# A decoder layer on one core: attention's transposes over four banks, block one's softmax after block zero's, and rooms for the raw weights of sevenfold chunks

## The chip, the cores and the metric

The kernel runs on one core of a Trainium2 chip. The metric is the device time of one execution in microseconds (us); less is better. TensorE is PE (its weight loads PEld), VectorE DVE, ScalarE ACT, GpSimd POOL, SyncE SP. DMAs are issued from SP's and ACT's queues.

## The reference

One layer of a hybrid decoder, 256 tokens of width 2048, float32. Cut to what matters:

```python
h = rmsnorm(x, norm_mix_pre)
xr, yr, q, k, v, g_rnn, g_attn = split(h @ w_in)
y_rnn = rg_lru(conv(xr)) * gelu(yr)
y_att = sliding_window_sink_attention(rope(q), rope(k), v, sinks)   # 32 heads of 64, 4 key heads
mix = sigmoid(g_rnn) * (y_rnn @ w_rnn_proj) + sigmoid(g_attn) * (y_att @ w_attn_proj)
x = x + rmsnorm(mix @ w_out, norm_mix_post)
u = square(relu(rmsnorm(x, norm_mlp_pre) @ w_mlp_up))               # 2048 -> 8192
x = x + rmsnorm(u @ w_mlp_down, norm_mlp_post)                      # 8192 -> 2048
```

The attention works in two blocks of 128 queries; block zero sees its own 128 keys, block one 256.

## The kernel before, in words

**Weights.** Every weight matrix comes in chunks of 128 x 2048, each as two halves of 128 x 1024 (512 KB). A float32 product is made of three single-pass products: a weight w is split into whi = w rounded (a cast on ACT, line 94) and wlo = w - whi (DVE, line 95), and so are the activations. The class Stream (lines 54 to 156) does this in the order of use. load_to (66 to 78) issues the raw halves from SP into a ring of WRAW = 4 tiles named wraw; split_to (80) splits them into rings of six whi and six wlo; ahead (138 to 140) keeps the splitting six halves and the loading four more ahead of the half that PE uses.

**Rooms.** A pool named big has 12 rooms of 128 x 2048 float32 with the tag U8. hT, h2T (four rooms each), x, the rooms of the scores, uT, acc and others take them in turn: a tile that asks for a room waits until the one that had it before is no longer used.

**Attention** (532 to 636), for four groups g of eight query heads. It is a generator: a pass of PE over weights calls pump, which moves it on to its next yield, so its small matmuls stand between the weight matmuls. scores (549 to 570) makes the products q.k, and on DVE adds the mask and takes the maximum of each tile. softmax (572 to 590) subtracts the maximum with the exponential on ACT (582, with an accumulating read) and scales on DVE (587). turn_probs (592 to 607) transposes the probabilities on PE (604), four to a PSUM bank, and ACT copies them out; there are two such banks (psm). Then come the products with v (630). In the order before, the scores of both blocks are made and masked first, and then softmax(0) and, after a yield, softmax(1).

**First norm** (433 to 449). r = 1/rms of the tokens is spread over the partitions by a matmul of ones with a diagonal (448, tile pr), and copied to rT. keys_values (515 to 528) calls it, rotates and turns the keys (tile pk).

**MLP.** The hidden width is done in two parts f = 0 and 1. In each, 16 pairs p of up-projection steps (a_pair or up_pair) and evacuate (1063) make uT, of which the pairs in SEVEN = (0, 2, ... 12) are kept in a special form of seven left operands (tiles "seven", pool pc). Then down (1092) makes the product with w_dn in two passes n of 1024 output columns. A chunk of a pair in SEVEN is a "sevenfold" chunk: four 128 x 128 by 512 products are made from seven instead of eight (a Winograd form). For that split_sums (114 to 136) forms sums of the raw weights on DVE: t (123), then two sums of 512 (125, 126), the two halves' whi and wlo, thi on ACT (129) and tlo on DVE (130). t, thi and tlo take big rooms. PE uses 21 matmuls of 512 columns for a sevenfold chunk and 24 for a plain one (1084); they alternate up to p = 12, then three plain ones end the pass. todo (980) is a list of up-projection steps that PE does ahead between the transposes of the second norm.

**End.** In the last pass (f = 1, n = 1) early (1190) adds acc, the sum of the earlier parts, to the four results of the sevenfold products: two on DVE and two on POOL. It also asks for x1, the residual, back from DRAM. between (1199) multiplies the finished columns by the gain g3, finish (1205) adds the last bank, squares (1214), norms, and writes out (1223, 1224).

The order of instructions on each engine comes from the tile framework's scheduler, with priorities, and from "pin", which keeps the program's order.

Of the kernel before, what the change touches and what calls it, by code (L numbers as in the profile page):

```python
# [30 lines left out]
NH, NKV, HD = 32, 4, 64  # L31
# [5 lines left out]
WRAW, WHALF, T2, HELD = 4, 6, 8, 4  # L37

SEVEN = (0, 2, 4, 6, 8, 10, 12)
# [14 lines left out]
class Stream:  # L54
# [11 lines left out]
    def load_to(self, n):  # L66
        while self.loaded < min(n, 2 * len(self.chunks)):
            j = self.loaded
            c = slice(j % 2 * 1024, j % 2 * 1024 + 1024)
            if j < 2 * EXTRA:  # L70
                if j % 2 == 0:
                    self.place = self.room(f"wraw{j}")
                t = self.place[:, c]
            else:
                t = self.pool.tile([P, 1024], F32, tag="wraw", bufs=WRAW, name=f"wraw{j}")
            self.nc.sync.dma_start(t, self.chunks[j // 2][:, c])
            self.raw[j] = t
            self.loaded += 1

# [57 lines left out]

    def ahead(self, j):
        self.split_to(j + AHEAD)
        self.load_to(max(2 * EXTRA, j + WHALF) + WRAW)  # L140

    def half(self, run_ahead=True):
        j = self.at
# [20 lines left out]
EXTRA = 5  # L164


def layer(tc, x, g_pre, pos_t, pos_row, inv_freq, vecs, sinks, gains, w_kv, w_q, w_xy, w_rg, w_g, w_rp, w_ap, w_out,
          w_up, w_dn, out):
    nc = tc.nc
# [8 lines left out]
    mm = nc.tensor.matmul  # L178
# [43 lines left out]
    def bank(pool, name):  # L222
        return pool.tile([P, 512], F32, tag=pool.name, name=name)
# [105 lines left out]
    def quarter(q):  # L329
        return slice(q * 512, q * 512 + 512)  # L330
# [13 lines left out]
    ident = const.tile([P, P], F32, name="ident")  # L344
# [3 lines left out]
    sq = const.tile([P, 4, TB, 4], F32, name="sqs")  # L348
    ones = const.tile([P, P], F32, name="ones")
# [80 lines left out]
    ws.ahead(ws.at - 1)  # L430
    r0, r0h = [], []
    rT = pa.tile([P, S], F32, name="rT")

    def first_norm():

        pr = bank(psm, "pr")
        spread = t2("spread")
        for tb in range(TB):
            r = rms(tb, 0)
            half = st[:, 16 + tb : 17 + tb]  # L440
            nc.vector.tensor_scalar(half, r, 0.5, None, ALU.mult)
            r0.append(r)
            r0h.append(half)
            for t in (cc, ss):
                nc.vector.tensor_scalar(t[:, tb], t[:, tb], r, None, ALU.mult)
            dg = spread[:, tb * P : tb * P + P]
            nc.vector.tensor_scalar(dg, ident, r, None, ALU.mult)
            mm(pr[:, tb * P : tb * P + P], ones, dg, start=True, stop=True)
        nc.scalar.copy(rT, pr[:, 0:S])

    pos_i = pa.tile([P, TB], I32, name="pos_i")
# [63 lines left out]
    def keys_values(banks):  # L515
        yield
        first_norm()
        for tb in range(TB):
            nc.scalar.activation(v_sb[:, tb, :], banks[tb][:, 256:512], AF.Copy, scale=r0[tb])
            k2 = t2("k2")  # L520
            k4 = k2.rearrange("p (g c d) -> p g c d", g=NKV, c=2)
            rope(banks[tb][:, 0:256], tb, NKV, [k4[:, :, 0, :], k4[:, :, 1, :]])
            yield
            ps = bank(psm, "pk")
            for g in range(NKV):
                nc.tensor.transpose(ps[:, g * P : g * P + P], k2[:, g * P : g * P + P], ident)
            nc.scalar.copy(kT[:, :, tb * P : tb * P + P], ps.rearrange("p (g t) -> p g t", g=NKV))
            yield

    yatt = []  # L530

    def attention(g, banks):

        qT = pa.tile([P, 4, S], F32, tag="qT", bufs=2, name=f"qT{g}")
        for tb in range(TB):
# [3 lines left out]
            ps = bank(psm, "pq")  # L539
# [6 lines left out]
        rooms, stats, tiles = {}, {}, {}  # L546
# [42 lines left out]

        pT = {}  # L590

        def turn_probs(tb):
            nk = 1 + tb
            per = 4 // nk
            if tb:
                room_p = flat(unit("pT", F32)).rearrange("p (n c) -> p n c", c=512)
            else:
                room_p = rooms[tb][:, 2:4, :]
            for par in range(2):
                for kb in range(nk):  # L600
                    ps = bank(psm, "pt")
                    for h in range(4):
                        s3, at = tiles[tb][h // per * 2 + par]
                        nc.tensor.transpose(ps[:, h * P : h * P + P], s3[:, h % per, kb * P : kb * P + P], ident)
# [20 lines left out]
        yield  # L625
# [213 lines left out]
    x1 = po.tile([P, TB, D], F32, name="x1")  # L839
# [40 lines left out]
    held = o_pass(mixT, banks, HELD)  # L880
# [208 lines left out]

    PLACE = {(0, 0): "Q4", (0, 1): "Cs", (1, 0): "P2", (1, 1): "Q3"}  # L1090

    def down(f, n, uT, held, order, finish, early, between=lambda p: None):
# [21 lines left out]
        for p in range(PAIRS - held):  # L1114
# [25 lines left out]
                        begun.add(b)  # L1140
            between(p)
        parts = [[ws.half(False) for i in range(2)] for p in range(held)]
        for name in order:
            for i in range(held):
                step(PAIRS - held + i, parts[i], (name,))
            finish(name, banks[PLACE[name]], ready[name])
        ws.ahead(ws.at - 1)

    for f in range(2):
# [38 lines left out]
        x1 = []  # L1188

        def early(ready):  # L1190
            for (tb, i), t in ready.items():
                c = quarter(2 * n + i)
                (nc.gpsimd if n and tb else nc.vector).tensor_tensor(t, t, acc[tb][:, c], ALU.add)
            if n == 1:
                for tb in range(TB):
                    x1.append(flat(unit(f"x1{tb}", F32)))
                    nc.scalar.dma_start(x1[tb], x1_away[tb])

        def between(p):
            if p in (3, 5, 7, 9):  # L1200
                tb, q = divmod((p - 3) // 2, 2)
                c = quarter(q)
                nc.vector.tensor_tensor(acc[tb][:, c], acc[tb][:, c], g3[:, c], ALU.mult)

        def finish(name, b, t):
            tb, i = name
            q = 2 * n + i
            c = quarter(q)
            a = acc[tb][:, c]
            nc.vector.tensor_tensor(a, b, t, ALU.add)  # L1210
# [3 lines left out]
            nc.scalar.activation(spare[:, c], a, AF.Square, accum_out=sq[:, 3, tb, q : q + 1])  # L1214
            nc.vector.tensor_tensor(t, a, g3[:, quarter(q)], ALU.mult)
            last[tb, i] = t
            if i == 0:
                return
            r = rms(tb, 3)
            for q in range(4):  # L1220
                c = quarter(q)
                g = acc[tb][:, c] if q < 2 else last[tb, q - 2]
                nc.vector.scalar_tensor_tensor(x1[tb][:, c], g, r, x1[tb][:, c], ALU.mult, ALU.add)
                (nc.scalar if q % 2 else nc.sync).dma_start(o_v[tb][:, c], x1[tb][:, c])

        n = 0
        down(f, n, uT, 2, order, finish, early)
        n = 1
        last = {}
        spare = flat(unit("spare", F32))  # L1230
        g3 = flat(unit("g3", F32))
        nc.scalar.dma_start(g3, gains[3].partition_broadcast(P))
        down(f, n, uT, 2, [(0, 0), (0, 1), (1, 0), (1, 1)], finish, early, between)
    ctx2.close()
    ctx.close()

# [71 lines left out]
```

## Time and profile before

| | |
|---|---|
| three runs | median 1517.41 us (1516.36 to 1518.62) |
| profiled execution | 1517.5 us |
| its span | 1515.7 us |
| weights from DRAM | 288.60 MB read, 195 GB/s over the span |
| granted TensorE clock | 1.00 in all stretches up to 1500 us |

A row of a group has the line, engine, operation, out<-in, shapes and count, then busy time and mean duration in ns, and last the idle time of that engine just before them with what ended most of it. A row of a timeline has start, duration, engine, line and operation, and in brackets the idle time before it and its releaser.

### The profile page before, as it was taken

How to read it: one execution, taken by the hardware profiler on the slowest of the kernel's cores; microseconds unless marked ns; L12 is line 12 of the kernel's file. 1: busy time of each engine (PE TensorE's matmuls, PEld its weight loads, DVE VectorE, ACT ScalarE, POOL GpSimd, SP SyncE). 2: the span in 40 equal slices, each digit the busy share in tenths (PEclk: the TensorE clock that was granted, in tenths of full speed). 3: DMA queues.
4: the chain of work that ended last, by engine and by line, in shares of the span. 5: the costliest groups of instructions: out<-in, count | busy, mean ns of one | idle time of the engine just before them, and what ended most of it. 6: DMA issues, size and time to landing. Idle time of an engine off the chain costs nothing.

```text
span 1515.7 us, 20016 instructions
## 1 busy us (share of the span) xinstructions
PE 1493.5 (99%) x7600; PEld 1259.8 (83%) x7600; DVE 1102.2 (73%) x1377; ACT 829.2 (55%) x1143; POOL 5.5 (0%) x11
## 2 busy tenths in 40 slices
PE   9999999999999999999999999999999999999996
PEld 7787778788888888888888888888888888888875
DVE  6666677858769966555667866798886666688897
ACT  6554654646566766443355655555454455555543
POOL 0000000000000000000000000000000000000001
PEclk9999999999999999999999999999999999999999
DMA  6645445465646565655764756566657555566564
GB/s 253 218 144 187 142 131 170 153 196 166 217 159 215 174 209 196 191 183 194 268 225 137 271 183 193 185 203 213 219 195 239 194 188 188 193 236 213 195 209 174
DMA packets 82895, 296.19 MB, mean 195 GB/s; under 512 B 9712, under 2 KB 9968, under 8 KB 81648
## 3 DMA queue, kind: packets, MB, share of 16 engines
q1 hardware_dynamic: 79056, 284.43, 57.4%
q10 hardware_dynamic: 3744, 10.50, 1.9%
q8 instruction: 59, 0.97, 0.2%
q14 instruction: 36, 0.29, 0.1%
HBM read 288.60 MB, written 6.29 MB: 195 GB/s over the span
## 4 chain that ended last, share of the span: by engine, by line
PE 82%; DVE 9%; DMA 4%; ACT 2%; issue 2%; DVEq 0%; SPq 0%; ACTq 0%
PE ps L256 21%; PE ps L254 11%; PE dQ L1084 4%; DMA wraw<-in_w_dn 4%; PE pp L294 4%; PE pp L296 4%; PE pp L298 4%; PE g L294 3%; DVE wlo L95 3%; PE g L298 3%; PE g L296 3%; PE s L1084 3%; PE dP L1084 2%; PE q L296 2%; PE q L298 2%; PE q L294 2%
## 5 line engine op out<-in xcount | busy, mean ns | idle before, releaser
L94 ACT CAST whi<-wraw 128x1024 fp32r<-128x1024 f32 x523 | 544.6, 1053 | 567.5 <-PE ps L256 123.7
L95 DVE TENSOR_TENSOR wlo<-wraw,whi 128x1024 fp32r<-128x1024 f32 x523 | 632.8, 1221 | 301.9 <-ACT whi L94 295.2
L256 PE MATMUL ps<-h2T,whi 128*128 128x512 f32 x960 | 223.9, 390 | 0.0
L256 PEld LDWEIGHTS ps<-h2T,whi 128*128 128x128 f32 x960 | 178.2, 188 | 35.6
L256 PE MATMUL ps<-hT,whi 128*128 128x512 f32 x512 | 121.3, 391 | 0.0
L254 PEld LDWEIGHTS ps<-h2T,wlo 128*128 128x128 f32 x960 | 119.1, 192 | 2.3
L254 PE MATMUL ps<-h2T,wlo 128*128 128x256 f32 x960 | 119.9, 283 | 0.0
L256 PEld LDWEIGHTS ps<-hT,whi 128*128 128x128 f32 x512 | 94.7, 188 | 20.1 <-issue 1.5
L1084 PE MATMUL dQ<-whi,uT 128*128 128x512 f32 x288 | 106.9, 389 | 0.0
L294 PE MATMUL g<-whi,hT 128*128 128x512 f32 x256 | 101.2, 395 | 0.0
L296 PE MATMUL g<-wlo,hT 128*128 128x512 f32 x256 | 100.0, 391 | 0.1
L298 PE MATMUL g<-whi,hT 128*128 128x512 f32 x256 | 99.8, 390 | 0.0
L254 PE MATMUL ps<-hT,wlo 128*128 128x256 f32 x512 | 64.9, 283 | 0.0
L254 PEld LDWEIGHTS ps<-hT,wlo 128*128 128x128 f32 x512 | 63.8, 191 | 1.2
L1084 PEld LDWEIGHTS dQ<-whi,uT 128*128 128x128 f32 x288 | 54.1, 188 | 11.2
L1084 PE MATMUL dQ<-wlo,uT 128*128 128x512 f32 x144 | 56.4, 391 | 1.2 <-DVE wlo L95 1.1
L294 PEld LDWEIGHTS g<-whi,hT 128*128 128x128 f32 x256 | 48.1, 188 | 10.6 <-issue 1.0
L298 PEld LDWEIGHTS g<-whi,hT 128*128 128x128 f32 x256 | 48.1, 188 | 10.2
L296 PEld LDWEIGHTS g<-wlo,hT 128*128 128x128 f32 x256 | 48.1, 188 | 9.9 <-DVE wlo L95 0.5
L1084 PE MATMUL dCs<-whi,uT 128*128 128x512 f32 x144 | 54.1, 389 | 0.0
L1084 PE MATMUL dP<-whi,uT 128*128 128x512 f32 x144 | 54.1, 389 | 0.0
L130 DVE TENSOR_TENSOR tlo<-t,thi 128x1536 fp32r<-128x1536 f32 x28 | 49.2, 1756 | 5.5 <-ACT thi L129 5.3
(280 smaller groups left out, 2462.1 us busy)
## 6 DMA issues: line engine op xcount, KB each, us to landing
wraw<-in_w_up SPq DMA_DIRECT2D x128, 512.0 KB, 4.1
wraw<-in_w_dn SPq DMA_DIRECT2D x128, 512.0 KB, 4.8
wraw<-in_w_g SPq DMA_DIRECT2D x64, 512.0 KB, 4.7
wraw<-in_w_xy SPq DMA_DIRECT2D x64, 512.0 KB, 4.5
wraw<-in_w_q SPq DMA_DIRECT2D x32, 512.0 KB, 4.4
wraw<-in_w_ap SPq DMA_DIRECT2D x32, 512.0 KB, 4.6
wraw<-in_w_rp SPq DMA_DIRECT2D x32, 512.0 KB, 4.1
wraw<-in_w_out SPq DMA_DIRECT2D x32, 512.0 KB, 4.9
```

Of the source, the lines that this page charges most:

```text
L94: self.pin(self.nc.scalar.copy(hi, src))
L95: self.pin(self.nc.vector.tensor_tensor(lo, src, hi.bitcast(F32), ALU.subtract))
L130: v.tensor_tensor(lo, t, hi.bitcast(F32), ALU.subtract)
L254: mm(ps[:, f, 1, :], w, a[:, 0, :], start=False, stop=j == 1 and k == 7)
L256: mm(ps[:, f].rearrange("p a b -> p (a b)"), w, a.rearrange("p a b -> p (a b)"), start=kt == 0, stop=j == 3 and k == 7)
L294: mm(banks[tb][n], a[:, 0, t], hi[:, n * 512 : n * 512 + 512], start=first, stop=False)
L296: mm(banks[tb][n], a[:, 0, t], lo[:, n * 512 : n * 512 + 512], start=False, stop=False)
L298: mm(banks[tb][n], a[:, 1, t], hi[:, n * 512 : n * 512 + 512], start=False, stop=last)
L1084: mm(b, a[x], w[y], start=not begun and i == 0, stop=tail and i == 2)
```

## The change

In Stream, the raw halves of sevenfold chunks (in self.sums) no longer come from the ring of four but from one big room for both halves, in all four passes of the down projection. ahead loads in such a way that the two halves of a sevenfold chunk go together. In the attention softmax(0) goes ahead of the scores of block one; in the first three groups the transposes of block zero come one step of the pump earlier, and block one's 16 go together, over four banks (a pair of banks and the two of psm); in the last group block zero's come later and block one's in two bundles. The spreading of r goes behind the transposes of the keys, in a function of its own. 30 instead of 26 up-projection steps stand ahead of the first turn of the second norm. In the last pass all four adds of early are on DVE, x1 comes back on SP's queue behind the last weights, in four pieces, g3 in two halves on ACT's queue, both in rooms of "seven" tiles no longer used; the squares are written to the PSUM bank itself.

```diff
-            if j < 2 * EXTRA:
+            if j < 2 * EXTRA or j // 2 in self.sums:
                 if j % 2 == 0:
                     self.place = self.room(f"wraw{j}")
                 t = self.place[:, c]
...
     def ahead(self, j):
         self.split_to(j + AHEAD)
-        self.load_to(max(2 * EXTRA, j + WHALF) + WRAW)
+        n = max(2 * EXTRA, j + WHALF) + WRAW
+
+        self.load_to((n + 1) // 2 * 2 + 2 if (n - 1) // 2 in self.sums else n)
...
+    def spread_out():
+        pr = bank(psm, "pr")
+        for tb in range(TB):
+            mm(pr[:, tb * P : tb * P + P], ones, spread[:, tb * P : tb * P + P], start=True, stop=True)
         nc.scalar.copy(rT, pr[:, 0:S])
...
         scores(0, 0, [bank(psm, "sc") for par in range(2)])
+        softmax(0)
         scores(1, 0, [bank(psb, "sc") for par in range(2)])
         if not last_group:
             scores(1, 1, two_banks("sc"))
-        softmax(0)
         yield
         if last_group:
             scores(1, 1, [bank(psb, "sc") for par in range(2)])
         softmax(1)
         yield
-        turn_probs(0)
         yield
-        yield
-        turn_probs(1)
-        yield
+        if last_group:
+            yield
+            turn_probs(0)
+            yield
+            yield
+            yield
+            turn_probs(1, (0,))
+            yield
+            turn_probs(1, (1,))
+            yield
+            yield
+        else:
+            turn_probs(0)
+            yield
+            yield
+            turn_probs(1, banks=two_banks("pt"))
+            yield
...
-    for q, n in enumerate((26, 6, 6, 6)):
+    for q, n in enumerate((30, 6, 6, 6)):
...
-                (nc.gpsimd if n and tb else nc.vector).tensor_tensor(t, t, acc[tb][:, c], ALU.add)
-            if n == 1:
-                for tb in range(TB):
-                    x1.append(flat(unit(f"x1{tb}", F32)))
-                    nc.scalar.dma_start(x1[tb], x1_away[tb])
+                nc.vector.tensor_tensor(t, t, acc[tb][:, c], ALU.add)
...
         def between(p):
-            if p in (3, 5, 7, 9):
+            if p in (0, 2):
+                g3.append(free_half(f"g3{p}"))
+                nc.scalar.dma_start(g3[-1], gains[3][p * 512 : p * 512 + 1024].partition_broadcast(P))
+            if p in (4, 6, 8, 10):
...
+        def residual_back():
+
+            for tb in range(TB):
+                for i in range(2):
+                    x1[tb, i] = free_half(f"x1{tb}{i}")
+                    with tc.issue_after(ws.load):
+                        ws.load = nc.sync.dma_start(x1[tb, i], x1_away[tb][:, i * 1024 : i * 1024 + 1024]).ins
```

More of the change, by code (lines that the diff above doesn't have):

```diff
@@ L75, in load_to @@
                 t = self.pool.tile([P, 1024], F32, tag="wraw", bufs=WRAW, name=f"wraw{j}")
-            self.nc.sync.dma_start(t, self.chunks[j // 2][:, c])
+            self.load = self.nc.sync.dma_start(t, self.chunks[j // 2][:, c]).ins
             self.raw[j] = t
@@ L432, in layer @@
     rT = pa.tile([P, S], F32, name="rT")
+    spread = t2("spread")
     def first_norm():
-        pr = bank(psm, "pr")
-        spread = t2("spread")
         for tb in range(TB):
@@ L445, in first_norm @@
                 nc.vector.tensor_scalar(t[:, tb], t[:, tb], r, None, ALU.mult)
-            dg = spread[:, tb * P : tb * P + P]
-            nc.vector.tensor_scalar(dg, ident, r, None, ALU.mult)
-            mm(pr[:, tb * P : tb * P + P], ones, dg, start=True, stop=True)
+            nc.vector.tensor_scalar(spread[:, tb * P : tb * P + P], ident, r, None, ALU.mult)
+    def spread_out():
+        pr = bank(psm, "pr")
+        for tb in range(TB):
+            mm(pr[:, tb * P : tb * P + P], ones, spread[:, tb * P : tb * P + P], start=True, stop=True)
         nc.scalar.copy(rT, pr[:, 0:S])
@@ L517, in keys_values @@
         first_norm()
+        keys = []
         for tb in range(TB):
             nc.scalar.activation(v_sb[:, tb, :], banks[tb][:, 256:512], AF.Copy, scale=r0[tb])
-            k2 = t2("k2")
-            k4 = k2.rearrange("p (g c d) -> p g c d", g=NKV, c=2)
+            keys.append(t2("k2"))
+            k4 = keys[tb].rearrange("p (g c d) -> p g c d", g=NKV, c=2)
             rope(banks[tb][:, 0:256], tb, NKV, [k4[:, :, 0, :], k4[:, :, 1, :]])
             yield
+        yield
+        yield
+        for tb in range(TB):
             ps = bank(psm, "pk")
             for g in range(NKV):
-                nc.tensor.transpose(ps[:, g * P : g * P + P], k2[:, g * P : g * P + P], ident)
+                nc.tensor.transpose(ps[:, g * P : g * P + P], keys[tb][:, g * P : g * P + P], ident)
             nc.scalar.copy(kT[:, :, tb * P : tb * P + P], ps.rearrange("p (g t) -> p g t", g=NKV))
-            yield
+        yield
+        spread_out()
+        yield
     yatt = []
@@ L590, in attention, with turn_probs @@
         pT = {}
-        def turn_probs(tb):
+        def turn_probs(tb, pars=(0, 1), banks=()):
             nk = 1 + tb
             per = 4 // nk
[L595 to L599, printed above, removed]
+            if pars[0] == 0:
+                rooms["p", tb] = (flat(unit("pT", F32)).rearrange("p (n c) -> p n c", c=512) if tb
+                                  else rooms[tb][:, 2:4, :])
+            room_p = rooms["p", tb]
+            banks = list(banks)
+            for par in pars:
                 for kb in range(nk):
-                    ps = bank(psm, "pt")
+                    ps = banks.pop(0) if banks else bank(psm, "pt")
                     for h in range(4):
@@ L620, in attention @@
         yield
-        turn_probs(0)
         yield
-        yield
-        turn_probs(1)
-        yield
+        if last_group:
[8 more added lines that the diff above has]
+            yield
+            yield
+        else:
+            turn_probs(0)
+            yield
+            yield
+            turn_probs(1, banks=two_banks("pt"))
+            yield
         for tb in range(TB):
@@ L1090, in layer, with down @@
     PLACE = {(0, 0): "Q4", (0, 1): "Cs", (1, 0): "P2", (1, 1): "Q3"}
-    def down(f, n, uT, held, order, finish, early, between=lambda p: None):
+    def down(f, n, uT, held, order, finish, early, between=lambda p: None, split=lambda: None):
         two = [pair(f"s{i}") for i in range(2)]
@@ L1142, in down @@
         parts = [[ws.half(False) for i in range(2)] for p in range(held)]
+        split()
         for name in order:
@@ L1187, in layer @@
             nc.scalar.dma_start(acc[tb], acc_away[tb])
-        x1 = []
+        x1, g3 = {}, []
         def early(ready):
@@ L1192, in early, with free_half @@
                 c = quarter(2 * n + i)
-                (nc.gpsimd if n and tb else nc.vector).tensor_tensor(t, t, acc[tb][:, c], ALU.add)
-            if n == 1:
-                for tb in range(TB):
-                    x1.append(flat(unit(f"x1{tb}", F32)))
-                    nc.scalar.dma_start(x1[tb], x1_away[tb])
-        def between(p):
-            if p in (3, 5, 7, 9):
-                tb, q = divmod((p - 3) // 2, 2)
-                c = quarter(q)
-                nc.vector.tensor_tensor(acc[tb][:, c], acc[tb][:, c], g3[:, c], ALU.mult)
+                nc.vector.tensor_tensor(t, t, acc[tb][:, c], ALU.add)
+        def free_half(name):
+            t = pc.tile([P, 2, 7, P], F32R, tag="seven", bufs=len(SEVEN), name=name)
+            return t.rearrange("p a b c -> p (a b c)")[:, 0:1024].bitcast(F32)
+        def between(p):
+            if p in (0, 2):
+                g3.append(free_half(f"g3{p}"))
+                nc.scalar.dma_start(g3[-1], gains[3][p * 512 : p * 512 + 1024].partition_broadcast(P))
+            if p in (4, 6, 8, 10):
+                tb, q = divmod((p - 4) // 2, 2)
+                c = quarter(q)
+                nc.vector.tensor_tensor(acc[tb][:, c], acc[tb][:, c], g3[0][:, c], ALU.mult)
+        def residual_back():
+            for tb in range(TB):
+                for i in range(2):
+                    x1[tb, i] = free_half(f"x1{tb}{i}")
+                    with tc.issue_after(ws.load):
+                        ws.load = nc.sync.dma_start(x1[tb, i], x1_away[tb][:, i * 1024 : i * 1024 + 1024]).ins
         def finish(name, b, t):
@@ L1213, in finish @@
                 return
-            nc.scalar.activation(spare[:, c], a, AF.Square, accum_out=sq[:, 3, tb, q : q + 1])
-            nc.vector.tensor_tensor(t, a, g3[:, quarter(q)], ALU.mult)
+            nc.scalar.activation(b, a, AF.Square, accum_out=sq[:, 3, tb, q : q + 1])
+            nc.vector.tensor_tensor(t, a, g3[1][:, quarter(i)], ALU.mult)
             last[tb, i] = t
@@ L1222, in finish @@
                 g = acc[tb][:, c] if q < 2 else last[tb, q - 2]
-                nc.vector.scalar_tensor_tensor(x1[tb][:, c], g, r, x1[tb][:, c], ALU.mult, ALU.add)
-                (nc.scalar if q % 2 else nc.sync).dma_start(o_v[tb][:, c], x1[tb][:, c])
+                y = x1[tb, q // 2][:, quarter(q % 2)]
+                nc.vector.scalar_tensor_tensor(y, g, r, y, ALU.mult, ALU.add)
+                (nc.scalar if q % 2 else nc.sync).dma_start(o_v[tb][:, c], y)
         n = 0
@@ L1229, in layer @@
         last = {}
[L1230 to L1233, printed above, removed]
+        down(f, n, uT, 2, [(0, 0), (0, 1), (1, 0), (1, 1)], finish, early, between, residual_back)
     ctx2.close()
```

## The prediction

> **What bounds the kernel now.** I read the page first, then a table of 25 us stretches, then for each stretch with idle TensorE the groups of PE with what ended their waits. In the table the columns are busy time and instructions of PE, PEld, DVE, ACT and POOL, granted clock, DMA share, GB/s.
>
> ```profile
> span 1515.7 us, 20016 instructions
> PE 1493.5 (99%) x7600; PEld 1259.8 (83%) x7600; DVE 1102.2 (73%) x1377; ACT 829.2 (55%) x1143; POOL 5.5 (0%) x11
> ```
>
> ```profile
> 25.00:50.00 25.00, 24.03 (x110) 19.11 (x109) 21.20 (x50) 19.99 (x35) 0.00 (x0) 1.00 0.48 173
> ...
> 150.00:175.00 25.00, 23.58 (x113) 17.36 (x114) 19.03 (x35) 18.42 (x50) 0.00 (x0) 1.00 0.32 102
> ...
> 200.00:225.00 25.00, 23.57 (x133) 18.82 (x132) 18.14 (x33) 15.53 (x47) 0.00 (x0) 1.00 0.31 99
> ...
> 250.00:275.00 25.00, 23.45 (x156) 19.83 (x156) 23.17 (x52) 13.40 (x32) 0.00 (x0) 1.00 0.31 101
> ...
> 800.00:825.00 25.00, 24.19 (x162) 21.87 (x161) 20.13 (x31) 15.01 (x27) 0.00 (x0) 1.00 0.29 92
> ...
> 1025.00:1050.00 25.00, 25.00 (x112) 20.68 (x111) 22.18 (x22) 14.31 (x14) 0.00 (x0) 1.00 0.63 198
> ...
> 1425.00:1450.00 25.00, 24.79 (x110) 20.20 (x109) 19.68 (x20) 12.11 (x13) 0.00 (x0) 1.00 0.70 239
> 1450.00:1475.00 25.00, 24.26 (x107) 19.79 (x106) 23.56 (x23) 14.09 (x14) 0.00 (x0) 1.00 0.61 201
> 1475.00:1500.00 25.00, 23.83 (x103) 18.75 (x103) 18.45 (x19) 8.91 (x9) 3.81 (x2) 1.00 0.59 210
> ```
>
> TensorE is idle 1515.7 - 1493.5 = 22.2 us. What the change can reach of it is 1.0 (25-50), 4.4 in three attention stretches (1.42, 1.43, 1.55), 0.8 (800-825), and 0.2 + 0.7 + 1.2 = 2.1 late in the down projection; much of the rest is the tail. The first down projection (1025-1050) has none, but its DVE is busy 22.2 of 25 us. The profiled execution took 1517.5 us, 1.8 more than its span and 0.1 above the median of the three runs (1517.41). The sum is made against 1517.5. Within 0.2% means within 3.0 us, about what a measurement of this kernel tells from no change.
>
> **Attention.** Rows of group 1, of ACT, DVE and PE:
>
> ```profile
> 158.29 0.39 ACT L582 ACTIVATE s<-s,stat 128x128 f32<-128x128 f32 x1
> ...
> 161.28 0.19 ACT L582 ACTIVATION_READ_ACCUMULATOR s<-s,stat 128x1 f32 x1
> ```
>
> ```profile
> 149.42 1.28 DVE L566 SCALAR_TENSOR_TENSOR s<-sc,mask 128x512 f32<-128x512 f32 x2
> 150.62 1.27 DVE L568 TENSOR_REDUCE stat<-s 128x4 f32<-128x512 f32 x2
> ...
> 161.94 1.29 DVE L587 TENSOR_TENSOR s<-s,stat 128x512 f32<-128x512 f32 x2
> ```
>
> ```profile
> 160.97 0.39 PE L294 MATMUL q<-whi,hT 128*128 128x512 f32 x1
> 162.78 1.23 PE L604 MATMUL pt<-ident,s 128*128 128x128 f32 x8 [1.42 <-DVE s L587]
> ```
>
> Before, block zero's exponentials start at 158.29, because DVE first masks and reduces all six tiles; eight of them with their reads take 3.2 us, and the scaled rows follow at 161.94. With softmax(0) ahead of block one's scores, DVE reaches it after one pair, at 151.8, the exponentials run about 152.4 to 156.6 (3.2 us and one weight cast of 1.05 between them), and the scaling comes behind block one's two mask pairs (2 x 2.4) and one wlo of 1.2, at 157.8: results at 158.5 and 159.15. But the transposes also move one weight half earlier: 12 matmuls and their share, 2.9 us, so PE stands at them at about 158.1 instead of 161. Of 1.42 us some 0.6 stays. So it goes in groups 1 and 2; in the last group the transposes come later than before, and its 1.55 goes. Group 0 waited for nothing and may lose 0.2. Gain 0.8 + 0.8 + 1.55 - 0.2 = 3.0. Block one's 16 transposes now go in bundles of 16 or 12 and 4 over four banks, not in fours: each insertion into the stream costs a little (in the row above eight last 1.23 and the next matmul starts 0.98 after them), and saving two per group gives an estimated 0.2 x 3. I take **3.4** (1 to 4.8).
>
> **The spread of r.** Two groups of waits, of 0-50 and of 800-825:
>
> ```profile
> L448 PE MATMUL pr<-spread,ones 128*128 128x128 f32 x4 | 0.9, 300 | 0.9 <-DVE spread L447 0.9
> ```
>
> ```profile
> L921 PE MATMUL ptr<-ident,h 128*128 128x128 f32 x32 | 4.6, 276 | 0.8 <-DVE h L915 0.7
> ```
>
> The pr matmuls go behind the keys' transposes, and r is out long before: **0.9** goes (0 to 0.9; ACT's copy of rT has no user near). Four up-steps more ahead of the first turn (30 instead of 26) are 4 x 0.11 = 0.45 us of work that PE does in its wait of 0.7: **0.45** (0 to 0.7). They are moved, not added.
>
> **Raw weights in rooms, first down projection (f = 0).** This is the costly part. A room that holds both raw halves comes from the big pool of 12; with the four rooms of h2T still live and five for uT, three are left for raw, t, thi and tlo of every seven. Worked out from the order in which the changed program allots them: from the fourth seven on, the raw weights of seven k+1 take the room of t of seven k, so their DMA waits for tlo of k, and t of k+1 takes the room of tlo of k. Behind that DMA on SP stand plain halves of the next pair. On DVE the order is wlo of the first half, t, the two halves of the sums, wlo of the second, tlo; whatever waits there holds the next pair's wlo too. Before, each raw half has a slot of the ring of four, free again after its own wlo. Rows of before for the steps of this loop (DVE, ACT, then the raw loads of 985-1060, with their time to landing):
>
> ```profile
> 1012.92 1.23 DVE L123 TENSOR_TENSOR t<-wraw,wraw 128x1024 f32<-128x1024 f32 x1 [0.70 <-DMA wraw<-in_w_dn]
> 1014.06 1.22 DVE L95 TENSOR_TENSOR wlo<-wraw,whi 128x1024 fp32r<-128x1024 f32 x1
> ...
> 1025.06 0.68 DVE L125 TENSOR_TENSOR wraw<-t,wraw 128x512 f32<-128x512 f32 x1
> ...
> 1030.86 1.76 DVE L130 TENSOR_TENSOR tlo<-t,thi 128x1536 fp32r<-128x1536 f32 x1 [0.37 <-ACT thi L129]
> ```
>
> ```profile
> 1025.90 2.95 ACT L94 CAST whi<-wraw 128x1024 fp32r<-128x1024 f32 x3 [2.71 <-DVE wraw L125]
> 1029.35 1.48 ACT L129 CAST thi<-t 128x1536 fp32r<-128x1536 f32 x1 [0.49 <-PE s L1084]
> ```
>
> ```profile
> L76 SPq DMA_DIRECT2D wraw<-in_w_dn x30: 327/328/328, 986.7 to 1059.2; - x30
> ...
> DMA to landing us min/median/max: 3.6/4.6/7.1
> ```
>
> ```profile
> 994.01 0.39 PE L1084 MATMUL s<-whi,seven 128*128 128x512 f32 x1
> ...
> 998.77 0.39 PE L1084 MATMUL dQ<-whi,uT 128*128 128x512 f32 x1
> ...
> 1004.21 0.39 PE L1084 MATMUL s<-whi,seven 128*128 128x512 f32 x1
> ```
>
> One turn of the loop: hand-over to SP 0.1; landing 3.8 (few loads beside it, so near the 3.6); whi 1.05 and hand-over 0.1; wlo 1.14 (1012.92 to 1014.06 is the pitch); t 1.14; L125 with the hand-over to ACT 0.84 (1025.06 to 1025.90); whi 1.0; thi 1.5 (1029.35 to 1030.86); tlo 1.75. Sum **12.4** us. PE spends 998.77 - 994.01 = 4.76 on a seven (21 matmuls of 0.227) and 5.44 on a pair, together 10.2 a turn. Bounds of the turn: 12.0 with wlo and t overlapped better and the landing 3.6; 13.7 when the second half lands at 7.1, since t needs both and starts 1.3 later.
>
> The last tlo not held by the loop (third seven) waits for PE's end of the second, 1004.21 + 4.76 = 1009.0; t 1.2, L125 0.84, whi 1.05, thi 1.5, tlo 1.75 put it at 1015.4. Four turns on, the seventh is at 1015.4 + 4 x 12.4 = 1065.0. By the changed order PE then has 76 matmuls of this pass left (93 from the seventh seven on, 17 placed ahead of its first tlo), 17.2 us, and ends at 1082.2. Before it ended at 994.01 + 6 x 10.2 + 93 x 0.2267 = 1076.3. Loss **5.9** (4T - 43.7 for a turn of T: 4.3 at 12.0, 11.1 at 13.7, nothing below 10.9). In the second pass the plain end of the first (17.2 us without sums) gives a lead of some 3.6 us; two full turns eat 4.4, and two whose rooms wait for the second wlo alone (2 us sooner) 0.2 each: loss **1.3** (0 to 4).
>
> On the price of a load the Trainium skill differs: SBUF — State Buffer, "The DMA setup-cost knee", fits a transfer by 2 us and its bytes at 436 GB/s, 3.2 us for 512 KB, and says itself that the fit is rough. By that a turn would be 11.8 and the first pass would lose 3.5. No row here lands under 3.6, so the sum stays with the rows.
>
> **The same in f = 1.** With h2T gone there are rooms enough: raw weights of seven k wait for PE's end of k-2, 15 us before they are used, against 6.2 us from issue to wlo and about 10 to tlo. I see 5 us of slack. The ring of four then serves plain halves alone, and the three late stalls of 2.1 us go: **1.9** (0 to 2.1).
>
> **The tail.**
>
> ```profile
> 1487.78 1.05 ACT L94 CAST whi<-wraw 128x1024 fp32r<-128x1024 f32 x1 [5.03 <-DMA wraw<-in_w_dn]
> ```
>
> ```profile
> 1497.76 2.38 DVE L1193 TENSOR_TENSOR t<-t,acc 128x512 f32<-128x512 f32 x2
> ...
> 1506.24 0.68 DVE L1210 TENSOR_TENSOR acc<-dP,t 128x512 f32<-128x512 f32 x1
> 1506.84 0.68 DVE L1210 TENSOR_TENSOR acc<-dQ,t 128x512 f32<-128x512 f32 x1
> ```
>
> ```profile
> 1504.51 0.39 PE L1084 MATMUL dQ<-whi,uT 128*128 128x512 f32 x1
> ```
>
> The last weights land late, DVE runs without a gap behind them, and the last add comes 1.94 us after PE's end at 1504.9. With the weights early DVE has 1.4 us less behind it (the add 0.5 after PE). POOL's two adds go to DVE: four at 0.65 instead of two at 1.19 cost 0.25. The loads of x1 move to SP behind the last weights, g3 comes in two halves on ACT's queue: both wait for PE points passed long before their use; at nothing, covered by 20 us of matmuls (3 us if x1 were late). **1.15** (-0.3 to 1.4).
>
> Sum: 1517.5 - 3.4 - 0.9 - 0.45 - 1.9 - 1.15 + 5.9 + 1.3 = 1517.5 - 7.8 + 7.2 = **1516.9**.
>
> **Rivals.** (A) *The loads are hidden anyway*: were a turn under 10.9, only the gains stay: 1517.5 - 7.8 = 1509.7; with a turn of 11.8, 1513.2. For it: the loads run alone on SP and DMA is busy 0.63. Against it: each step of the loop has its row, and only landing and hand-overs can shrink. (B) *The loop is longer*, the end on the other side: the second half's landing, not wlo, starts t. Above a turn of 12.9 the whole is slower by 0.2%: 4 x 12.9 - 43.7 = 7.9 and some 2.9 in the second pass are 10.8 - 7.8 = 3.0. At 13.7 it is 11.1 + 4 - 7.8 = 7.3: 1524.8. For it: the median landing of 4.6 with two to four loads in flight, and a longest of 7.1. Against it: fewer are in flight now. (C) *The attention does not do what it says*: the transposes go one half earlier and the wait only moves with them. The 3.0 stay: 1519.9, and with a turn of 12.6 it is past 0.2%. For it: DVE is busy 18 to 23 of 25 us there.
>
> **How the numbers follow.** Forecast 0.42 (own range 1514.0 to 1520.0); A 0.24; B 0.23; C 0.11. Faster is A and the low end of the forecast, 0.28; same is the rest of the forecast but its high end, and half of C, 0.39; slower is B, the other half of C and that high end, 0.33. Best bounds (turn 12.0, all gains at their upper end) give 1517.5 - 9.9 + 4.3 = 1511.9, A alone 1509.7, B 1524.8. The range 1511.0 to 1524.0 leaves out the ends of A and B.
>
> **What would show it.** In the changed profile: PE idle in 1030-1085 with waits ended by DVE tlo and whi, SP's raw loads one after each tlo, turns of 12.4 from tlo to tlo; idle of 1425-1500 gone; pt waits near 0.6 in two groups and nothing in the last; the last add within 0.7 us of PE's end. The forecast is wrong if turns follow PE's 10.2, or if f = 1 shows waits of its own.

## The result and the profile after

The changed kernel takes 1538.55 us (median of four, 1536.86 to 1539.43), the kernel before 1516.88 in the same session (1514.79 to 1518.62): a ratio of 1.0152, interval 1.014 to 1.0164. It is slower by 21.7 us. The forecast was 1516.9, with a range up to 1524.

The head of the page of the changed kernel, and eight of the stretches of 25 us in which PE is idle (the columns are those of the table before):

```profile
span 1537.6 us, 19996 instructions
PE 1501.8 (98%) x7600; PEld 1262.4 (82%) x7600; DVE 1102.2 (72%) x1379; ACT 827.1 (54%) x1143; POOL 1.7 (0%) x9
```

```profile
100.00:125.00 25.00, 22.88 (x113) 17.76 (x113) 16.51 (x28) 19.26 (x50) 0.00 (x0) 1.00 0.38 130
...
150.00:175.00 25.00, 22.77 (x127) 18.78 (x125) 20.09 (x35) 17.62 (x49) 0.00 (x0) 1.00 0.39 130
...
225.00:250.00 25.00, 22.93 (x102) 17.06 (x101) 10.66 (x12) 9.75 (x13) 0.00 (x0) 0.93 0.54 184
...
275.00:300.00 25.00, 23.55 (x135) 18.70 (x133) 21.18 (x34) 18.53 (x38) 0.00 (x0) 1.00 0.53 172
...
1025.00:1050.00 25.00, 23.40 (x101) 18.48 (x100) 17.62 (x16) 10.85 (x10) 0.00 (x0) 1.00 0.48 161
1050.00:1075.00 25.00, 22.80 (x91) 17.62 (x90) 20.57 (x19) 12.07 (x12) 0.00 (x0) 0.93 0.47 155
...
1100.00:1125.00 25.00, 22.70 (x91) 17.80 (x90) 19.37 (x18) 11.41 (x11) 0.00 (x0) 0.93 0.50 170
...
1450.00:1475.00 25.00, 22.86 (x99) 17.99 (x97) 17.50 (x18) 10.20 (x10) 0.00 (x0) 1.00 0.55 204
```

The same work leaves PE idle 35.8 us instead of 22.2, and PE is *busy* 8.3 us longer. So not all of the loss is waiting: three of the stretches have a mean granted clock of 0.93 (the last section). What PE waited for, from the list of its waits (total us, times, longest):

```profile
PE pt L615 <- ACT pT L617: 6.2, 3, 2.2
PE dP L1108 <- DVE wlo L95: 4.3, 7, 0.8
PE dP L1108 <- ACT whi L94: 4.0, 4, 1.4
PE pt L615 <- DVE s L597: 1.7, 3, 0.8
...
PE pk L534 <- DVE k L513: 1.6, 1, 1.6
```

The waits of pt for the scaled rows fell from 4.4 to 1.7 us, as was meant. A new one stands beside them, for ACT's copies pT, and it is larger. The spread's wait is now pk's. And the down projection, which had next to none in its first part, waits for whi and wlo.

To see where the time is lost, set the start of the same PE instruction in both traces side by side. The first product of the recurrent stage, behind the attention, was at 301.83 and is at 306.38; the first sevenfold product of the down projection was at 994.01 and is at 998.20; that of its second pass

```profile
1076.29 0.39 PE L1084 MATMUL s<-whi,seven 128*128 128x512 f32 x1
```

in the trace before, and in the trace after

```profile
1089.34 0.39 PE L1108 MATMUL s<-whi,seven 128*128 128x512 f32 x1
```

The last pass began at 1418.86 and begins at 1438.61; PE ended at 1504.9 and ends at 1526.7; the span's rest behind it is 10.9 us against 10.8. So the attention (with the spread before it) costs 4.6 us, the second norm gives back 0.4, the first pass of f = 0 costs 8.9, the second 6.7 (found at the start of the last pass, 19.75 - 13.05), the last pass 2.0, the tail 0.1. The large parts are f = 0's two passes and the attention.

### The profile page after: what moved, and what is told of

It is laid out like the page before. It is cut to its first block, busy times and chain, and to the rows that moved or that the text cites. A ratio compares the mean times of both kernels' runs of the same rounds, so it can differ in the third digit from the quotient of the medians.

```text
span 1537.6 us, 19996 instructions
## 1 busy us (share of the span) xinstructions
PE 1501.8 (98%) x7600; PEld 1262.4 (82%) x7600; DVE 1102.2 (72%) x1379; ACT 827.1 (54%) x1143; POOL 1.7 (0%) x9
## 4 chain that ended last, share of the span: by engine, by line
PE 79%; DVE 8%; DMA 6%; ACT 4%; issue 2%; SPq 0%; ACTq 0%; DVEq 0%
PE ps L258 21%; PE ps L256 11%; DMA wraw<-in_w_dn 5%; PE dQ L1108 4%; PE pp L298 4%; PE pp L300 4%; PE pp L296 4%; PE g L296 3%; PE g L300 3%; PE g L298 3%; PE s L1108 3%; PE dP L1108 2%; ACT whi L94 2%; DVE wlo L95 2%; PE o L300 2%
## 5 line engine op out<-in xcount | busy, mean ns | idle before, releaser
L300 PEld LDWEIGHTS g<-whi,hT 128*128 128x128 f32 x256 | 48.1, 188 | 10.2
```

The costliest lines, as they stand in the source:

```text
L300: mm(banks[tb][n], a[:, 1, t], hi[:, n * 512 : n * 512 + 512], start=False, stop=last)
```

## The experiments

Each was compared with the kernel before on the same chip; in these sessions its median was 1514.5 to 1515.5 us. The theory: three separate causes, namely the attention's fourth bank, the loop through the rooms in f = 0, and SP's order in f = 1. The rivals: that ACT is late by itself in the attention, and that the down projection loses by its later start or by loads that collide.

**The attention alone.** The attention's hunks of the diff, nothing else.

> The kernel before with only the attention's part of the change (softmax of block zero ahead, the transposes moved and over four banks). In the trace of the whole change the stretch up to the first matmul of the recurrent stage ended 4.6 us later than before. Theory (the fourth bundle of block one's transposes shares a tile with the first and waits for ACT's copy, and that copy stands on ACT behind a weight cast that waits for its load): the same 4 to 5 us here, 1520.5 to 1522, with three waits of about 2 us of PE for ACT's pT in the trace. Rival (the loss comes from the pr matmuls moved behind the keys and from there on, not from the transposes): no more than 1 us from before.

1520.88 us, ratio 1.0042 (1.0027 to 1.0057), 5.4 us slower; PE waits 6.1 us in three waits for pT. The theory holds, and the loss is in these hunks. Rows of ACT, then of PE, in group 0 of the whole change:

```profile
112.77 1.05 ACT L94 CAST whi<-wraw 128x1024 fp32r<-128x1024 f32 x1
115.96 1.04 ACT L94 CAST whi<-wraw 128x1024 fp32r<-128x1024 f32 x1 [2.14 <-DMA wraw<-in_w_q]
116.91 2.04 ACT L617 COPY pT<-pt 128x512 f32<-128x512 f32 x4
```

```profile
114.21 1.47 PE L615 MATMUL pt<-ident,s 128*128 128x128 f32 x12
117.54 0.66 PE L615 MATMUL pt<-ident,s 128*128 128x128 f32 x4 [1.86 <-ACT pT L617]
```

Two of the four banks are the halves of one pair tile. In program order the copy of the first half stands ahead of the transposes into the second, and the dependency is kept for the tile: four of the transposes, which PE takes last, wait until ACT has copied the first four. It is not the place in the program by itself, for the transposes into the two banks of psm stand behind the same copy there, and twelve of the sixteen run without a wait. ACT in turn stands at a cast whose raw weights land only at 115.9, and the copies, whose data are there, stand behind that cast on ACT and run at 116.91, when it is done. The copy needs nothing of that load, yet it waits for it, and PE with it.

**The same with the copies last.** In turn_probs:

```diff
+            turned = []
             for par in pars:
                 for kb in range(nk):
...
-                    t = room_p[:, par * nk + kb, :]
-                    nc.scalar.copy(t, ps)
-                    pT[tb, par, kb] = t
+                    turned.append((par, kb, ps))
+            for par, kb, ps in turned:
+                t = room_p[:, par * nk + kb, :]
+                nc.scalar.copy(t, ps)
+                pT[tb, par, kb] = t
```

> The attention's part alone, but with all transposes of a call issued ahead of their copies, so that no transpose waits for a copy of the same call. Theory: the 6.2 us of waits for pT and the slow stretch of the clock behind one of them go (some 7.5 us against the attention part alone), what is left are waits of 1.7 us for the scaled rows against 4.4 before: 1513.5 to 1515.5. Rival (ACT's lateness is what counts, and whatever reads its copies next takes the wait over): the products with v wait instead, 1518 to 1521.

1511.88 us, ratio 0.9981 (0.997 to 0.9992): 3.6 us faster than before and 9.0 faster than with the copies between. That is 1.6 us below the lower end of what was expected; why it is so much is open. Its PE and ACT rows in group 0:

```profile
113.64 1.91 PE L606 MATMUL pt<-ident,s 128*128 128x128 f32 x16
...
120.93 1.08 PE L647 MATMUL po<-s,v_sb 128*64 128x512 f32 x4
```

```profile
115.34 1.05 ACT L94 CAST whi<-wraw 128x1024 fp32r<-128x1024 f32 x1 [2.10 <-DMA wraw<-in_w_q]
116.30 2.04 ACT L610 COPY pT<-pt 128x512 f32<-128x512 f32 x4
```

ACT is as late as before, by the same 2.1 us behind the same load. All 16 transposes run in one go, and the products with v come at 120.93, when the copies are long done. So it was the tile's order and not ACT's lateness by itself: the rival falls.

**The rooms alone.** Stream's hunks and the last pass of the diff, nothing else.

> The kernel before with the rooms for raw weights in all four passes of the down projection and the last pass as changed; attention, spread of r and up-steps as before. Theory (loop of 12.7 us a turn against 10.2 of PE in the first f, waits in the second f): 8.9 + 6.7 + 2 = some 17.5 us more than before, 1533 to 1536. Rival (part of the loss in the down projection comes from its later start or from the attention): under 1528.

1532.15 us, ratio 1.0116 (1.0101 to 1.0131), 16.7 us slower. With the attention's 5.4 this makes 22.1, against the whole change's 21.7: the two add up.

**Rooms in the second f alone.**

```diff
+        self.roomy = {i for i in sums if i >= len(chunks) - 32}
...
-            if j < 2 * EXTRA or j // 2 in self.sums:
+            if j < 2 * EXTRA or j // 2 in self.roomy:
```

(and the same name in ahead; the last pass stays as changed.)

> As rooms alone, but in the first f all raw halves come from the ring of four as before; only the last two passes (f = 1) use rooms. Theory: the first down projection runs without waits as before and the loss of 15.6 us there is gone; what stays is that of the second f, 1517 to 1520. Rival (rooms cost by themselves, through SP's order and loads that collide): over 1524.

1518.91 us, ratio 1.0026 (1.0015 to 1.0036): 3.5 us slower than before, 13.2 faster than rooms everywhere. In its trace the passes of f = 0 have no wait and start as before (993.76 and 1076.04). That settles where the 13 us are; the next two ask by what.

**More free rooms in f = 0.** uT of f = 0 in four rooms, then in three, so that four and five rooms instead of three are left for raw, t, thi and tlo; part of the MLP's first half is overwritten and so left out. The edit for four rooms (for three, the 4 is a 3):

```diff
-        rooms = [unit(f"uT{f}{i}") for i in range((PAIRS - len(SEVEN) + 1) // 2)]
+        rooms = [unit(f"uT{f}{i}") for i in range((5, 4)[f == 0])]
...
-                    uT[q] = rooms[i // 2][:, 2 * (i % 2) : 2 * (i % 2) + 2]
+                    uT[q] = rooms[i // 2 % len(rooms)][:, 2 * (i % 2) : 2 * (i % 2) + 2]
```

> Rooms alone, but in the first f the activations uT take four big rooms instead of five (the ninth plain pair overwrites the first one's, so that part of the first half of the MLP is left out), so raw, t, thi and tlo of a sevenfold chunk turn over four rooms instead of three. Raw weights of seven k+1 then wait for the second wlo of seven k, about 1.9 us before its tlo. Theory (the loop through the rooms sets the first f's time): turns of 12.7 - 1.9 = 10.8 us, losses of about 2 us in each of the two passes instead of 8.9 and 6.7, so 1532.2 - 11 = 1521, with turns of 10.8 in the trace. Rival (SP's order and colliding loads set it): no shorter than 1529.

> The same with three rooms for uT in the first f (more plain pairs overwritten, that part of the MLP left out) and five free ones. No room is then asked for before it has long been left. Theory: no loop, turns of PE's 10.2, the first f as before, and 1518 to 1520 as with rooms in the second f alone. Rival (SP's order and colliding loads): no shorter than 1529.

Four rooms free: 1525.82 us (ratio 1.0071, 1.0049 to 1.0092; two executions). Five: 1517.92 (1.002, 1.001 to 1.0031), the time of rooms in the second f alone. Here are tlo of the first pass, all from DVE: those of the whole change (three rooms) from the third seven on, below them the same with four rooms, and then three of those with five:

```profile
1017.63 1.76 DVE L130 TENSOR_TENSOR tlo<-t,thi 128x1536 fp32r<-128x1536 f32 x1 [0.16 <-ACT thi L129]
1030.34 1.76 DVE L130 TENSOR_TENSOR tlo<-t,thi 128x1536 fp32r<-128x1536 f32 x1 [0.25 <-ACT thi L129]
1043.01 1.76 DVE L130 TENSOR_TENSOR tlo<-t,thi 128x1536 fp32r<-128x1536 f32 x1
1055.71 1.76 DVE L130 TENSOR_TENSOR tlo<-t,thi 128x1536 fp32r<-128x1536 f32 x1
1068.39 1.76 DVE L130 TENSOR_TENSOR tlo<-t,thi 128x1536 fp32r<-128x1536 f32 x1 [0.15 <-ACT thi L129]
```

```profile
1013.80 1.76 DVE L130 TENSOR_TENSOR tlo<-t,thi 128x1536 fp32r<-128x1536 f32 x1
1023.61 1.76 DVE L130 TENSOR_TENSOR tlo<-t,thi 128x1536 fp32r<-128x1536 f32 x1 [0.15 <-ACT thi L129]
1035.23 1.76 DVE L130 TENSOR_TENSOR tlo<-t,thi 128x1536 fp32r<-128x1536 f32 x1
1046.51 1.76 DVE L130 TENSOR_TENSOR tlo<-t,thi 128x1536 fp32r<-128x1536 f32 x1 [0.15 <-ACT thi L129]
1057.32 1.76 DVE L130 TENSOR_TENSOR tlo<-t,thi 128x1536 fp32r<-128x1536 f32 x1 [0.16 <-ACT thi L129]
```

```profile
1021.15 1.76 DVE L130 TENSOR_TENSOR tlo<-t,thi 128x1536 fp32r<-128x1536 f32 x1 [0.16 <-ACT thi L129]
1031.05 1.76 DVE L130 TENSOR_TENSOR tlo<-t,thi 128x1536 fp32r<-128x1536 f32 x1 [0.15 <-ACT thi L129]
1040.71 1.76 DVE L130 TENSOR_TENSOR tlo<-t,thi 128x1536 fp32r<-128x1536 f32 x1
```

With three rooms the turns are 12.71, 12.67, 12.70 and 12.68 us, one like the other, as of a loop that waits for nothing but itself; with four 9.8, then 11.6, 11.3 and 10.8; with five 9.9 and 9.7, faster than PE's 10.2, so that DVE gets ahead. The time follows the rooms step by step: the loop through the rooms is the cause in f = 0. With four rooms the run was 5 us longer than expected. Its trace shows where: the first pass takes 83.4 us where it took 82.3 before, but the second 87.5 where it took 82.1, so that 5.4 us are lost there and not the 2 expected. At its start DVE's t waits 3.38 us for raw weights (at 1080.22), and ACT's whi later 6.90 us (at 1096.09). What holds these loads up stays open.

**Rooms in the second f, SP in order.** The loads of f = 1 get the framework's mark that keeps program order:

```diff
-            self.load = self.nc.sync.dma_start(t, self.chunks[j // 2][:, c]).ins
+            i = self.nc.sync.dma_start(t, self.chunks[j // 2][:, c])
+            if j // 2 >= len(self.chunks) - 32:
+                self.order(i)
+            self.load = i.ins
```

> Rooms in the second f alone, with SP held to the order of use for the loads of that f, so that the raw weights of p = 6 no longer stand behind plain halves of p = 9 that wait for a wlo. Theory (that wait on SP makes the stall of 2.8 us at p = 6 of the last pass): the stall goes and the time is 1515.5 to 1516.5. Rival (the loads land late because they collide, whatever the order): 1518 to 1520 with a wait of over 1.5 us somewhere in the pass.

1514.24 us, ratio 0.9995 (0.9985 to 1.0004), 1.3 us below the lower end of what was expected, and without the wait at p = 6. A wait of 1.1 us for u, at the start of the down projection of f = 1, is new. So the loss in f = 1 was an order. In the run with rooms in the second f alone, ACT and PE show it at p = 6 of the last pass:

```profile
1439.04 1.05 ACT L95 CAST whi<-wraw 128x1024 fp32r<-128x1024 f32 x1
1447.40 1.05 ACT L95 CAST whi<-wraw 128x1024 fp32r<-128x1024 f32 x1 [7.31 <-DMA wraw<-in_w_dn]
```

```profile
1452.83 0.50 PE L1087 MATMUL dP<-whi,seven 128*128 128x512 f32 x1 [1.65 <-ACT whi L95]
1454.10 0.50 PE L1087 MATMUL dP<-wlo,seven 128*128 128x512 f32 x1 [0.76 <-DVE wlo L96]
```

and DVE and SP what stood ahead:

```profile
1441.99 1.22 DVE L96 TENSOR_TENSOR wlo<-wraw,whi 128x1024 fp32r<-128x1024 f32 x1
```

```profile
1443.24 0.82 SPq L77 DMA_DIRECT2D wraw<-in_w_dn  x2
```

The room for the raw weights of p = 6 is free once PE is through the sevenfold product of p = 2, at 1428.81 + 4.76 = 1433.6. Its load is issued only at 1443.2, because on SP a plain half of p = 9 stands ahead of it and, by the ring of four, waits for the wlo of p = 5, which ends then (1441.99 + 1.22).

**The spread alone.** The hunks of first_norm and keys_values.

> The kernel before with the spread of r moved behind the keys' transposes, and nothing else. Theory (the keys' transposes meet the wait that the pr matmuls had, since the rotation is DVE's work behind the same norm): no change, 1515 to 1516, with a wait of pk of about 1.5 us for DVE in place of pr's 0.9. Rival (as forecast): 0.9 us less.

1515.5 us, ratio 1.0001 (0.9992 to 1.0011). PE's wait for the spread is gone, and in its list stands

```profile
PE pk L532 <- DVE k L511: 1.2, 1, 1.2
```

**Thirty up-steps alone.** The one number, 26 to 30.

> The kernel before with 30 instead of 26 up-steps ahead of the first turn, and nothing else. Theory: PE's wait of 0.7 us for h shrinks to 0.3, 0.4 us less, hardly to be told in the time. Rival: the wait stays and the ring's halves come later, 1 us more.

1515.35 us, ratio 1.0004 (0.9995 to 1.0014). The wait of ptr for h is 0.3 instead of 0.7 us; the time can't tell it.

**The last pass alone.** The diff's hunks from down on, with the ring for all raw halves.

> The kernel before with the last pass as changed (adds on DVE, g3 in halves, x1 on SP behind the last weights), raw weights from the ring everywhere. Theory (x1's four loads collide with the last weight halves, which makes the stall of 1.6 us near the end of the changed kernel): 1 to 2 us more than before. Rival (that stall belongs to the rooms): within 0.5 us of before, or less by the DVE work that no longer waits.

1516.75 us, ratio 1.001 (1.0001 to 1.0019): 1.8 us slower, which is in the theory's numbers. But its trace has no wait of PE over 0.2 us in the last pass, so the theory's mechanism is not there, and where the 1.8 us lie I can't tell. So the stall of 1.6 us near the end of the changed kernel does not come from the last pass by itself. Nor do the rooms and the last pass together bring it: the run with the rooms alone has both, and no wait of PE there. In the changed kernel the last plain half is issued at 1507.6, with x1's four loads behind it from 1507.9, and takes 7.8 us to land. What brings the stall stays open.

**The parts that pay.** The attention with copies last, 30 up-steps, rooms and order in f = 1, the last pass; then the same with SP's order held in the last pass alone (len(self.chunks) - 16 instead of - 32).

> The attention's part with transposes ahead of their copies, 30 up-steps, rooms for raw weights in the second f alone with SP's loads there in order of use, and the last pass as changed; spread of r as before, first f from the ring. Theory (the gains lie in different stages and add up): 1514.9 - 3 (attention) - 0.4 (up-steps) - 2 (second f) = 1509.5, between 1508 and 1511.5, and no wait of PE over 1.2 us behind the first 20 us. Rival (one of the stages takes back what another gives, by loads that come later): 1512 or more.

> As parts_that_pay, but SP's loads are held to the order of use only in the last pass, where the wait of p = 6 was. In parts_that_pay PE waited 2.8 us at the first sevenfold product of the second f for u, which stood on DVE behind the tlo of a chunk loaded in order; rooms in the second f alone did not have this wait. Theory (holding the order in the pass before makes that wait): it goes, 2 to 3 us less than parts_that_pay, 1507 to 1508.5. Rival (the wait comes from the rooms or from the up-steps): 1509.5 to 1511.

1509.98 us (ratio 0.9971, 0.996 to 0.9982), and 1508.49 us (0.9956, 0.9943 to 0.997), 6.0 us faster than the kernel before and some 30 faster than the changed one. The first of the two had a wait of 2.8 us for u at the start of the down projection of f = 1, which the second has not: an order that helps one pass made a new wait in the other. In time the second gains 1.5 us on the first, less than the 2 to 3 expected, and the two intervals overlap, so this rests on the lists of waits. The whole list of the second:

```profile
PE pt L612 <- DVE s L593: 1.7, 3, 0.8
PE ptr L381 <- DMA x<-in_x: 1.6, 1, 1.6
PE warm L372 <- DVE ones L356: 1.1, 1, 1.1
PE pr L454 <- DVE spread L453: 0.9, 1, 0.9
PE kv L402 <- DVE wlo L115: 0.4, 1, 0.4
PE ptr L944 <- DVE h L938: 0.3, 1, 0.3
PE dQ L1107 <- DVE tlo L134: 0.2, 1, 0.2
```

## Why the prediction was wrong

*Attention (forecast 3.4 us gained, measured 5.4 lost): the step that failed.* The working weighed when the scaled rows are ready against when PE gets to the transposes, and there it was right in the sum: 1.7 us of these waits stay, though in the last group (1.45) and not in groups 1 and 2. But it counted "four banks" as four free places. That the bundle in the second half of the pair tile waits for a copy of the first half stands in the changed program; the part on the attention named no new wait at all. In place of the gain, PE waits three times some 2 us for ACT's copies (6.2 in all), and the slow clock behind the third costs about 1.7 more. With the copies last the same hunks gain 3.6, close to the 3.4 forecast, though the waits that stay are in other groups than forecast. The rival that the attention does not do what it says was there, priced at the 3.0 that would stay, and for another reason.

*The loop in f = 0 (forecast 5.9 + 1.3, measured 8.9 + 6.7).* The mechanism was right, and the turn nearly: 12.7 against 12.4 (the first half landed in 4.0 us where 3.8 was taken), with tlo of the third seven done at 1019.4, 21.2 us behind the start of the pass, against 21.4 forecast. The Trainium skill (SBUF — State Buffer, "The DMA setup-cost knee") gives 3.2 us for that load by its fit, an estimate; the 4.0 measured decide. Four turns of 0.3 more are 1.2 us of the first pass's 3.0. The other 2 lie behind the last tlo: with it done at 1070.15, PE's 17.2 us would have ended at 1087.35, but the pass ended at 1089.34. PE waited 0.76 and 0.23 there for wlo and whi of the plain pairs and had 78 matmuls left where 76 were counted; the last half microsecond I can't place. The term that was mis-sized most is the lead in the second pass. It was put at 3.6 us, without a working; the first tlo of that pass was done at 1091.2, and PE, which starts the pass at 1089.34, wants it 13 matmuls later, at 1092.3: 1.1 us. SP issued six raw halves between 1070.2 and 1074.7, behind the last tlo of the first pass, and they took 3.9 to 10.7 us to land, with a median of 8.4, where the forecast took 3.8: casts of ACT wait 4.41 and 1.16 us for them at 1077.05 and 1079.26, and t of the next pass 1.26 at 1082.94. To this extent rival B was right. From that lead the two full turns took 13.8 and 12.75 us, and a stretch of slow clock follows at 1104 (last section).

*f = 1 (forecast 1.9 gained, measured 2.0 lost, 3.5 by the run with rooms in that f alone, which has the changed last pass too).* The three old stalls went, and one came at p = 6 (1.37 and 0.77 us in the changed kernel, 1.65 and 0.76 in that run), and in the changed kernel another near the end. Waits of its own in f = 1 were the prediction's sign of being wrong. The slack of 5 us was taken from when the room is free. It overlooked that the load stands in SP's queue behind one whose place is not yet free.

*Spread (0.9) and up-steps (0.45).* The first wait moved to the keys' transposes, which need DVE's rotation behind the same norm. The second shrank as forecast, and is below what the time shows.

*Tail (1.15).* It did not come: the last weights were late again, by 1.6 us of PE's waits, and the last add is once more at 1.9 us behind PE's end (1528.6 against 1526.7). The mechanism was right, though: with SP in order in the second f the last weights are early, and the last add

```profile
1503.15 0.68 DVE L1229 TENSOR_TENSOR acc<-dQ,t 128x512 f32<-128x512 f32 x1
```

comes at PE's end of 1503.1; the span's rest behind PE's end is 9.1 us there instead of 10.8.

In the attention and in f = 1 the range was too narrow for the same reason: each term was bounded by its durations, and none for a queue whose head waits.

## What to carry to other kernels

Before trusting a buffer that is "free", look at what it shares a tile with and what stands ahead of its transfer in the queue: here ACT's copies waited for a load that they don't need, and SP's load for a place that was another's. Where a ring is taken from a common pool, write out which tile each next one replaces; if a load takes the place of the last product made from the load before, nothing is ahead any more, and the stage runs at the length of that loop. Issue all writers of a shared tile before its first reader.

## What the runs showed of the hardware

A wait can cost more than its length. In group 2 of the changed kernel's attention PE waited 2.07 us, and then (windows of 2 us, the third last column is the granted clock)

```profile
228.00:230.00 2.00, 1.00 (x6) 0.88 (x7) 1.23 (x1) 2.00 (x5) 0.00 (x0) 0.97 0.85 258
230.00:232.00 2.00, 2.00 (x6) 1.60 (x5) 0.00 (x0) 0.41 (x1) 0.00 (x0) 0.50 0.97 385
232.00:234.00 2.00, 2.00 (x7) 1.59 (x7) 0.00 (x0) 0.21 (x1) 0.00 (x0) 0.68 0.61 231
```

the clock was 0.50 for some 3.4 us, with a matmul each 0.43 us instead of 0.23: about 1.7 us lost, all of it counted as busy. The same came twice in f = 0, at 1056 and 1104, behind two waits close together (1.14 and 0.53; 0.88 and 0.77). Three times that is 5 of the 8.3 us by which PE is busier. Waits of 1.86 and 2.23 us in the two groups before did not bring it. In the last pass, two waits of 1.64 and 0.76 us brought it in the run with the rooms alone, and two of 1.65 and 0.76 in the run with rooms in the second f alone did not; what decides is not shown. The Trainium skill (TensorE: Matmul & The Clock Gate, "Part 1: The HAM clock gate") says that the clock halves after an idle window of about 3.4 us that runs by itself, and that a busy window of the same length brings it back. The 3.4 us of the slow stretch above agree with it, though in the run with the rooms alone one lasted almost 7 us. But no wait here was as long as the page's window: waits of about 2 us were enough, and not every time.

The rest of the 8.3 us may lie in the waits themselves, of which the list has 29 in the changed kernel and 12 before. At 1101.94 the row has a wait of 0.88, but PE's starts lie 1.27 apart there, 1.04 more than the usual 0.23. Some 0.2 us for each of 17 more waits are 3.4 us, an estimate from this row and the next (0.16 and 0.26 lost beyond the wait).
